# Even layer of a two-layer decoder: recurrent part first, value and gated outputs through DRAM, last head beside the output projection

## The chip, the cores and the metric

The kernel runs on one core of a Trainium2 chip. The metric is device time of one launch in microseconds (us), the median of several runs. Five engines work side by side, each through its own instruction stream in order: TensorE (PE, with its weight loads PEld), VectorE (DVE), ScalarE (ACT), GpSimd (POOL), and SyncE (SP), which here issues DMAs.

## The reference, cut to what matters

```python
# even layer, x: (1, 1024, 1024) f32
a_x, a_g, b_q, b_k, b_v, b_g = split(x @ w_in)           # 6 x 1024 columns
a_h = rg_lru(causal_dwconv(a_x, conv_w, conv_b), ...)    # gates: 8 blocks of 128x128, then a scan over the sequence
y_a = a_h * silu(a_g)
o_b = stick_breaking(b_q, b_k, b_v)                      # 8 heads of 128, strictly causal
y_b = o_b * silu(b_g)
x = layer_norm(alpha * x + concat([y_a, y_b]) @ w_out)
# odd layer: sliding-window attention, gated, output projection, layer norm (not touched by the change)
```

## The kernel before, in words

Every large product is made in three float32r passes (`mm3`, lines 109 to 112: high x high, high x low, low x high), so each operand exists as a high and a low tile. A "split" is an ACT copy that rounds to the high tile and a DVE subtraction that leaves the low one (`split_psum`, line 117). Weight pieces of 256 KB come by `load_piece` (line 91): one DMA on SP, then two POOL operations (lines 102 and 103) that split it. There are 3 raw and 5 split buffers for pieces.

The input x arrives transposed in 16 DMAs (`load_x`, line 124) and stays as 16 of the 24 `slots` of 4 KB per partition. The even layer has three stages:

1. **Attention**, heads n = 0 to 7 (`attn_all`, line 240). A head is 12 units (row tile i, key half g). `u_stage` makes the logits in a PSUM bank "z", ACT two sigmoids, DVE a reversed product scan and a product; `t_stage` transposes the weights on PE and splits them; `v_stage` multiplies them by the head's values. After each unit the loop pumps a *filler*: a generator of projection matmuls for the next head (`head_proj`, line 231: k, q, on even heads the values of two heads, then the gate), at a rate given by hand (line 325). `v_proj` (line 211) computes values 256 columns wide, for two heads at a time. Head 7's filler is `lru_proj(0)`.
2. **Recurrent part (LRU)**, blocks f = 0 to 7 (lines 468 to 473). `lru_main(f)` (line 402) makes two gates on PE, then Tanh, Exp, Sqrt on ACT, products on POOL and DVE, and a scan on DVE; `lru_proj(f+1)` (line 370: two projections, the depthwise convolution on DVE at line 381) is its filler.
3. **Output projection** (`out_proj`, line 483): for each half dm of the columns, 16 weight pieces e (8 of y_b, 8 of y_a), each against 8 row tiles s, accumulated in all 8 PSUM banks (3 "pj", 2 "z", 2 "tr", 1 "pv"). Ahead of it every y is split (lines 586 to 606; for y_b 1 to 7 the high part is made on POOL, line 590). The residual `xpre` (4 MB) is loaded at line 582.

The program text isn't the order on the engines: a planner of the framework takes every instruction with its dependences, buffers and a cost model, and writes each engine's order from a simulated run, first ready and earliest in the text first. Releases of buffers become semaphore waits. The profile's granted clock tells which of TensorE's two levels (1.2 and 2.4 GHz) holds.

Of the kernel before, what the change touches and what calls it, by code (L numbers as in the profile page):

```python
# [18 lines left out]
P = 128  # L19
# [33 lines left out]
def trunk(ctx, tc, x, xT_in, w_even, w_even_v, w_even_out, w_gate, lru_vec,  # L53
# [70 lines left out]
    def load_x(hf, dps):  # L124
        for dp in dps:
            raw = slot(f"xraw{hf}{dp}", F32)
            h = slot(f"xh{hf}{dp}", F32R)
            l = slot(f"xl{hf}{dp}", F32R)
            for c in range(2):
                x_dma.append(nc.sync.dma_start(raw[:, c, :], xT_in[hf, dp, :, c, :]))  # L130
                order(x_dma[-1], x_dma[-2] if len(x_dma) > 1 else None)
                nc.scalar.copy(h[:, c, :], raw[:, c, :])
                nc.vector.tensor_tensor(out=l[:, c, :], in0=raw[:, c, :], in1=h[:, c, :].bitcast(F32),  # L133
                                        op=ALU.subtract)
            xth[hf, dp], xtl[hf, dp] = h, l
# [45 lines left out]
    YB = {"vh": 3, "vl": 3, "wt": 2}  # L181
# [29 lines left out]
    def v_proj(pr, eng="pool", after=None):  # L211
        pieces = [load_piece(w_even_v[pr, g], f"v{pr}_{g}", eng=eng, after=after) for g in range(4)]
        for j in range(2):
            vt[2 * pr + j] = tuple(yt(f"v{c}", [P, NS, P], f"v{c}{2 * pr + j}") for c in "hl")
        for st in range(NS):
            ps = bank("pj", f"pjv_{pr}_{st}")[:, :256]
            for d in range(ND):
                wh, wl = pieces[d // 2]
                c = (d % 2) * 256
                xh, xl = xs(st // 4, d)  # L220
                c2 = (st % 4) * P
                mm3(ps, xh[:, c2:c2 + P], xl[:, c2:c2 + P], wh[:, c:c + 256], wl[:, c:c + 256],
                    d == 0, d == ND - 1)
                if d < ND - 1:
                    yield C_256
            for j in range(2):
                vh, vl = vt[2 * pr + j]
                split_psum(ps[:, j * P:(j + 1) * P], vh[:, st, :], vl[:, st, :])
            yield C_256

    def head_proj(n):
        yield from proj_ftile(w_even, 8 + n, f"k{n}", evac_qk("k", n), (1, 0))
        yield from proj_ftile(w_even, n, f"q{n}", evac_qk("q", n), (1, 0))
        if n % 2 == 0:
            yield from v_proj(n // 2)
        yield from proj_ftile(w_even, 16 + n, f"g{n}", evac_gate(("b", n)))

    rate = [0.0]

    def attn_all():  # L240
# [50 lines left out]
        def v_stage(n, j):  # L291
# [110 lines left out]
    def lru_main(f):  # L402
        st = lru_state[f]
        gh, gl = load_piece(w_gate[f], f"gate{f}", cols=256)
        if f < 6:
            ya = yt(YA[f], [P, 2, HALF], f"ya{f}", F32)
        else:
            if f == 6:
                ya67.append(yt("wt", [P, 2, 2, HALF], "ya67", F32))
            ya = ya67[0][:, f - 6]  # L410
        ytile["a", f] = ya
# [23 lines left out]
        for hf in range(2):  # L435
# [6 lines left out]
            nc.vector.tensor_tensor(out=ya[:, hf, :], in0=xc, in1=st["gg", hf], op=ALU.mult)  # L442
        yield

    getk = w_ftile(w_even, 8, "k0", "act", lazy=True)
    getq = w_ftile(w_even, 0, "q0", "act", lazy=True)
    load_x(0, [0])
    getk(0)
    load_x(0, [1])
    getk(4)  # L450
    load_x(0, [2, 3])
    getq(0)
    getq(4)
    load_x(1, range(4))
    for hf in range(2):
        for _ in proj_half(getk, hf, "k0", evac_qk("k", 0)):
            pass
        for _ in proj_half(getq, hf, "q0", evac_qk("q", 0)):
            pass
    for _ in v_proj(0, "act", x_dma[-1]):  # L460
# [6 lines left out]

    for f in range(8):
        if f + 1 < 8:
            fill.add(lru_proj(f + 1))  # L470
        for _ in lru_main(f):
            fill.pump(20.8 / 4)
        fill.drain()
# [5 lines left out]
    ACC = ["pv", "pj", "pj", "pj", "z", "z", "tr", "tr"]  # L479
# [3 lines left out]
    def out_proj(w_src, es, yh, n_tail, tail_piece, lnp, gb, after, name, final):  # L483
# [100 lines left out]
    yhl = {}

    def split_y(key, mk, pool_h=False):
        raw = ytile[key]
        h, l = mk(0, f"yh{key[0]}{key[1]}"), mk(1, f"yl{key[0]}{key[1]}")
        if pool_h:
            nc.gpsimd.tensor_scalar(out=fl(h), in0=fl(raw), scalar1=1.0, scalar2=0.0, op0=ALU.mult, op1=ALU.add)  # L590
        else:
            nc.scalar.copy(fl(h), fl(raw))
        nc.vector.tensor_tensor(out=fl(l), in0=fl(raw), in1=fl(h).bitcast(F32), op=ALU.subtract)
        yhl[key] = (h, l)
# [3 lines left out]
    for f in range(8):
        if f < 4:
            split_y(("a", f), lambda i, nm: slot(nm, F32R))  # L600
        else:
            if f == 4:
                ysp = yt("wt", [P, 2, 2, HALF], "yhla4")
                split_y(("a", f), lambda i, nm: ysp[:, i])
            else:
                split_y(("a", f), lambda i, nm, f=f: yt(YSPLIT[f][i], [P, 2, HALF], nm))

    def yh_even(e, s):
        h, l = yhl[("b", e - 8) if e >= 8 else ("a", e)]
        c = (s % 4) * P  # L610
        return h[:, s // 4, c:c + P], l[:, s // 4, c:c + P]
# [232 lines left out]
    for p in range(PAIRS):  # L844
        split_y(("o", p), lambda i, nm: slot(nm, F32R))
# [62 lines left out]
```

## Time and profile before

| | us |
|---|---|
| median of 3 runs | 1294.53 (1293.71 to 1295.31) |
| span of the profiled execution | 1294.7 |
| PE / PEld busy in it | 1259.2 / 1077.1 |
| DVE / POOL / ACT busy in it | 792.5 / 566.5 / 563.7 |

The page gives no other time of the profiled execution than its span. PE's matmuls overlap each other in the pipeline (one lasts 0.39 us while the next starts 0.23 us later), so a stretch in which PE is "busy" throughout can still run more or fewer matmuls; the number of matmuls in a stretch (x...) tells how fast it went.

### The profile page before, as it was taken

To read this page: it belongs to the slowest core of one execution; us is meant where nothing else is said; L and a number is where in the kernel's file an instruction comes from. 1 tells how busy PE (TensorE), PEld (TensorE's weight loads), DVE (VectorE), ACT (ScalarE), POOL (GpSimd) and SP (SyncE) were. 2 spreads that over 40 slices of the span, in tenths; PEclk is the share of its full clock that TensorE was granted. 3 is DMA by queue.
4 is the path that set the end of the run, shared out by engine and by line. 5 is a ranking of instruction groups with operands and counts; after the bars stand their busy time and mean duration, and the time that the engine had idled before them with its cause. 6 is when DMAs were issued, how large, how long until landed. Compare 5 with 4: busy or idle time off the path is not lost.

```text
span 1294.7 us, 18487 instructions
## 1 busy us (share of the span) xinstructions
PE 1259.2 (97%) x6656; PEld 1077.1 (83%) x6656; DVE 792.5 (61%) x1693; ACT 563.7 (44%) x1219; POOL 566.5 (44%) x695
## 2 busy tenths in 40 slices
PE   7999999999999999999998899999999999999997
PEld 6988988898889888888776688888788888887886
DVE  6266455645564559577777931126457877778467
ACT  4134333333333335565556700013357777778400
POOL 0332243314322422556657763536445555556440
PEclk9999999999999999999999899999899999999999
DMA  6211011101110110111111052210111111111122
GB/s 204 58 41 33 25 49 34 33 17 50 33 34 24 50 37 13 37 46 46 44 49 41 25 219 64 70 29 26 49 33 33 34 34 34 33 34 40 35 90 98
DMA packets 33643, 64.15 MB, mean 50 GB/s; under 512 B 3984, under 2 KB 5392, under 8 KB 33296
## 3 DMA queue, kind: packets, MB, share of 16 engines
q1 hardware_dynamic: 32976, 61.92, 15.8%
q8 instruction: 53, 0.87, 0.3%
q10 hardware_dynamic: 576, 1.05, 0.3%
q14 instruction: 38, 0.31, 0.1%
HBM read 58.76 MB, written 4.19 MB: 49 GB/s over the span
## 4 chain that ended last, share of the span: by engine, by line
PE 80%; DVE 11%; ACT 4%; issue 3%; POOL 1%; DMA 1%; POOLq 0%; ACTq 0%; DVEq 0%
PE ope L110 4%; PE ope L112 4%; PE ope L111 4%; PE tr L283 2%; PE pjv L112 2%; PE pjv L111 2%; PE pjv L110 2%; PE pj_g L112 2%; PE pj_g L110 2%; PE pj_g L111 2%; PE pj_q L110 2%; PE pj_q L111 2%; PE pj_q L112 2%; PE pj_k L111 2%; PE pj_k L112 2%
## 5 line engine op out<-in xcount | busy, mean ns | idle before, releaser
L264 ACT ACTIVATE C<-z 128x512 f32<-128x512 f32 (+3 forms) x96 | 47.4, 494 | 130.2 <-DVE z L261 77.0
L756 POOL TENSOR_SCALAR S<-S,sm 128x256 f32<-128x256 f32 (+1 forms) x128 | 59.9, 482 | 77.8 <-DVE sm L754 30.0
L751 ACT ACTIVATE S<-S,sm 128x256 f32<-128x256 f32 (+1 forms) x128 | 62.6, 490 | 57.1 <-DVE sm L747 55.3
L501 ACT ACTIVATE rs<-mv,eps_t 128x1 f32<-128x1 f32 x16 | 4.7, 295 | 183.4 <-DVE mv L500 183.4
L492 DVE SCALAR_TENSOR_TENSOR xpre<-xpre,ope 128x512 f32<-128x512 f32 x16 | 10.8, 681 | 107.0 <-PE ope L112 107.0
L110 PE MATMUL pjv<-wh_v,xh 128*128 128x256 f32 x256 | 73.3, 286 | 0.0
L112 PE MATMUL pjv<-wh_v,xl 128*128 128x256 f32 x256 | 72.4, 283 | 0.0
L111 PE MATMUL pjv<-wl_v,xh 128*128 128x256 f32 x256 | 72.4, 283 | 0.0
L312 POOL TENSOR_TENSOR yb<-pvt,yb 128x128 f32<-128x128 f32 x32 | 15.8, 492 | 126.2 <-DVE pvt L311 110.0
L273 DVE TENSOR_TENSOR_SCAN C<-C,C,one 128x512 f32<-128x512 f32 x32 | 41.7, 1302 | 41.7 <-ACT C L264 41.7
L273 DVE TENSOR_TENSOR_SCAN C<-C,one 128x512 f32<-128x512 f32 (+1 forms) x64 | 54.7, 854 | 16.4 <-ACT C L264 16.3
L118 ACT CAST wt<-tr 128x512 fp32r<-128x512 f32 (+3 forms) x96 | 46.6, 486 | 40.7 <-PE tr L283 38.9
L275 DVE TENSOR_TENSOR B<-B,C 128x512 f32<-128x512 f32 (+3 forms) x96 | 57.3, 597 | 10.2 <-ACT pvt L309 0.5
L261 DVE TENSOR_TENSOR z<-z,mask 128x128 f32<-128x128 f32 x64 | 18.8, 296 | 67.6 <-PE z L259 65.7
L102 POOL TENSOR_SCALAR wh_g<-wr_g 128x512 fp32r<-128x512 f32 x16 | 10.7, 668 | 111.3 <-PE pjv L112 42.6
L110 PE MATMUL pj_k<-xh,wh_k 128*128 128x512 f32 x128 | 52.7, 412 | 5.6 <-DVE wh_k L105 5.6
L119 DVE TENSOR_TENSOR wt<-tr,wt 128x512 fp32r<-128x512 f32 (+3 forms) x96 | 52.6, 549 | 7.9 <-ACT wt L118 7.6
L110 PE MATMUL pj_ag<-xh,wh_ag 128*128 128x512 f32 x128 | 51.8, 405 | 5.7 <-DVE xc L381 5.7
L110 PE MATMUL ope<-wh_e,yhb 128*128 128x512 f32 x128 | 51.2, 403 | 6.2 <-DVE gg L395 3.8
L110 PE MATMUL pj_oq<-x1h,wh_oq 128*128 128x512 f32 x128 | 52.8, 412 | 0.0
L111 PE MATMUL pj_k<-xl,wh_k 128*128 128x512 f32 x128 | 51.2, 400 | 1.3 <-DVE xl L133 1.3
L110 PE MATMUL pj_q<-xh,wh_q 128*128 128x512 f32 x128 | 52.0, 406 | 0.1
(300 smaller groups left out, 4541.0 us busy)
## 6 DMA issues: line engine op xcount, KB each, us to landing
wr_e<-in_w_even_out_dram SPq DMA_DIRECT2D x32, 256.0 KB, 2.6
xraw<-in_xT_dram SPq DMA_DIRECT2D x16, 256.0 KB, 5.0
wr_v<-in_w_even_v_dram SPq DMA_DIRECT2D x16, 256.0 KB, 2.6
wr_g<-in_w_even_dram SPq DMA_DIRECT2D x16, 256.0 KB, 2.6
wr_ax<-in_w_even_dram SPq DMA_DIRECT2D x16, 256.0 KB, 2.6
wr_ag<-in_w_even_dram SPq DMA_DIRECT2D x16, 256.0 KB, 2.6
xpre<-in_x_dram SPq DMA_DIRECT2D x8, 512.0 KB, 8.2
wr_oq<-in_w_odd_dram SPq DMA_DIRECT2D x16, 256.0 KB, 2.6
```

Of the source, the lines that this page charges most:

```text
L110: nc.tensor.matmul(ps, wh, xh, start=start, stop=False)
L111: nc.tensor.matmul(ps, wh, xl, start=False, stop=False)
L112: nc.tensor.matmul(ps, wl, xh, start=False, stop=stop)
L118: nc.scalar.copy(h, ps)
L119: nc.vector.tensor_tensor(out=l, in0=ps, in1=h.bitcast(F32), op=ALU.subtract)
L261: nc.vector.tensor_tensor(out=z[:, W - P:W], in0=z[:, W - P:W], in1=mask, op=ALU.add)
L264: nc.scalar.activation(C[:, :W], z[:, :W], AF.Sigmoid, scale=-SC)
L273: nc.vector.tensor_tensor_scan(cr, cr, one.broadcast_to([P, W]), init, ALU.mult, ALU.mult)
L275: nc.vector.tensor_tensor(out=B[:, :W], in0=B[:, :W], in1=C[:, 1:W + 1], op=ALU.mult)
L283: nc.tensor.transpose(tr[:, t * P:(t + 1) * P], B[:, t * P:(t + 1) * P], ident)
L751: nc.scalar.activation(Sb[:, j, lo:], Sb[:, j, lo:], AF.Exp, bias=nm[:, j:j + 1], accum_out=den[:, j:j + 1])
L756: nc.gpsimd.tensor_scalar(out=Sb[:, j, lo:], in0=Sb[:, j, lo:], scalar1=rec[:, j:j + 1], scalar2=0.0, op0=ALU.mult, op1=ALU.add)
```

## The change

The even layer is turned round. It starts with x and half of the value weights (now 512 columns wide, 8 loads of 256 KB, split on ACT and DVE in slots) and computes the values of heads 0 to 3 for row tiles 0 to 3 in four banks, as x arrives. Then come `lru_proj(0)` and the eight LRU blocks; their filler is `lru_proj(f+1)` and, 12 tiles in all, the other value tiles (`VT`), for block 7 the projections of head 0. Values go, split, to DRAM scratch (16 stores of 512 KB); y_a is split per half and stored (16 of 512 KB). Then the attention: every head's filler is k, q, gate of the next head; `load_v` fetches its values in 16 DMAs of 64 KB (rows of 512 bytes). y_b is split per half as it comes; heads 0 to 4 store it (10 of 512 KB), 5 to 7 keep it. In head 7 the 16 halves of y_a are loaded into the slots that x left, and the filler is `early_out`: 10 pieces against row tiles 0 to 2 of the first half of the output projection, in the three "pj" banks. The projection then loads those 10 pieces again for row tiles 3 to 7, and does the other 6 pieces for all; y_b 0 to 4 are loaded ahead of it.

```diff
-    def load_x(hf, dps):
...
+    def load_x(hf, d):
+        dp, c = d // 2, d % 2
...
+        raw = wt_(("kh", "kl")[c], f"xraw{hf}{d}", F32)
+        x_dma.append(nc.sync.dma_start(raw, xT_in[hf, dp, :, c, :]))
+        order(x_dma[-1], x_dma[-2] if len(x_dma) > 1 else None)
+        h, l = xs(hf, d)
+        nc.scalar.copy(h, raw)
+        nc.vector.tensor_tensor(out=l, in0=raw, in1=h.bitcast(F32), op=ALU.subtract)
-    YB = {"vh": 3, "vl": 3, "wt": 2}
+    YB = {"vh": 2, "vl": 2, "wt": 2}
-    def v_proj(pr, eng="pool", after=None):
...
+    vst = [[tc.dram_tile([P, 2, 4, P], F32, name=f"vst{q}{st}") for st in range(NS)] for q in range(2)]
+    def load_wv(q, d):
+        raw = wt_(("qh", "ql")[d % 2], f"wvraw{q}{d}", F32)
+        x_dma.append(nc.sync.dma_start(raw, w_even_v[q, d]))
...
+        hl = wv[q, d] = slot(f"wv{q}{d}", F32R)
+        nc.scalar.copy(hl[:, 0, :], raw)
+        nc.vector.tensor_tensor(out=hl[:, 1, :], in0=raw, in1=hl[:, 0, :].bitcast(F32), op=ALU.subtract)
+    def v_evac(ps, q, st):
+        hl = yt(("vh", "vl")[st % 2], [P, 2, HALF], f"vhl{q}{st}")
+        split_psum(ps, hl[:, 0, :], hl[:, 1, :])
+        nc.sync.dma_start(vst[q][st].rearrange("p a h f -> p a (h f)"), hl.bitcast(F32))
+    def v_tiles(q, sts):
+        for st in sts:
+            ps = bank("pv", f"pjv{q}_{st}")
+            for d in range(ND):
+                v_mm(ps, q, st, d)
+                yield C_512
+            v_evac(ps, q, st)
+    def load_v(n):
+        vt[n] = tuple(yt(f"v{c}", [P, NS, P], f"v{c}{n}") for c in "hl")
         for st in range(NS):
+            for i in range(2):
+                nc.sync.dma_start(vt[n][i][:, st, :].bitcast(F32), vst[n // 4][st][:, i, n % 4, :])
     def head_proj(n):
...
-        if n % 2 == 0:
-            yield from v_proj(n // 2)
+    def split_y_half(key, hf, raw, keep):
+        hl = slot(f"yhl{key[0]}{key[1]}{hf}", F32R) if key[0] == "b" else \
+            yt(("vh", "vl")[hf], [P, 2, HALF], f"yhla{key[1]}{hf}")
+        nc.scalar.copy(hl[:, 0, :], raw)
+        nc.vector.tensor_tensor(out=hl[:, 1, :], in0=raw, in1=hl[:, 0, :].bitcast(F32), op=ALU.subtract)
+        if keep:
+            yhl[key + (hf,)] = hl
+        else:
+            yst[key + (hf,)] = tc.dram_tile([P, 2, HALF], F32, name=f"yst{key[0]}{key[1]}{hf}")
+            nc.sync.dma_start(yst[key + (hf,)], hl.bitcast(F32))
@@ attn_all
                     if n + 1 < SB_HEADS:
+                        load_v(n + 1)
                         fill.add(head_proj(n + 1))
-                        rate[0] = (31.2 if (n + 1) % 2 else 52.0) / 12
+                        rate[0] = 31.2 / 12
                     else:
-                        decay()
-                        fill.add(lru_proj(0))
-                        rate[0] = 20.8 / 12
+                        for hf in range(2):
+                            for f in range(8):
+                                load_y(("a", f), hf, slot(f"yla{f}{hf}", F32R))
+                        fill.add(early_out())
+                        rate[0] = 20.4 / 12
@@ lru_main
-            nc.vector.tensor_tensor(out=ya[:, hf, :], in0=xc, in1=st["gg", hf], op=ALU.mult)
+            nc.vector.tensor_tensor(out=gg, in0=xc, in1=gg, op=ALU.mult)
+            split_y_half(("a", f), hf, gg, False)
+    EARLY = [13, 0, 1, 2, 3, 4, 5, 6, 7, 14]
+    LATE = [8, 9, 10, 11, 12, 15]
+    for d in range(ND):
+        load_x(0, d)
+        load_wv(0, d)
+    ps = [bank(VB[st], f"pjv0_{st}") for st in range(4)]
+    for d in range(ND):
+        for st in range(4):
+            v_mm(ps[st], 0, st, d)
...
+    VT = [(0, (4, 5)), (0, (6, 7)), (1, (0,)), (1, (1, 2)), (1, (3,)), (1, (4,)), (1, (5, 6)), (1, (7,))]
+    for f in range(8):
+        q, sts = VT[f]
+        if f == 2:
+            for d in range(ND):
+                load_wv(1, d)
+        fill.add(v_tiles(q, sts))
+        if f + 1 < 8:
+            fill.add(lru_proj(f + 1))
+        else:
+            load_v(0)
+            fill.add(head_proj(0))
...
-    ACC = ["pv", "pj", "pj", "pj", "z", "z", "tr", "tr"]
+    ACC = ["pj", "pj", "pj", "z", "z", "tr", "tr", "pv"]
@@ out_proj: dm == 0 goes on from the three early banks
+                for ei, group in enumerate(early[1:]):
+                    for idx, e in enumerate(group):
+                        wh, wl = load_piece(w_src[dm, e], f"{name}{dm}_{e}")
+                        for s in range(NS):
+                            if ei == 0 and s in early[0]:
+                                continue
...
-    for n in range(8):
-        split_y(("b", n), lambda i, nm: slot(nm, F32R), n > 0)
...
```

## Rows read from the trace of the kernel before

**Rows 1.** The page: busy time per engine, and the span in 40 slices.
```profile
PE 1259.2 (97%) x6656; PEld 1077.1 (83%) x6656; DVE 792.5 (61%) x1693; ACT 563.7 (44%) x1219; POOL 566.5 (44%) x695
...
PE   7999999999999999999998899999999999999997
...
PEclk9999999999999999999999899999899999999999
```

**Rows 2.** PE in order of time: last half projections, then values of head 0.
```profile
26.21 0.39 PE L110 MATMUL pj_k<-xh,wh_k 128*128 128x512 f32 x1
...
31.66 0.28 PE L110 MATMUL pjv<-wh_v,xh 128*128 128x256 f32 x1
...
34.53 0.63 PE L257 MATMUL z<-kh,qh 128*128 128x512 f32 x2
```

**Rows 3.** Busy time (instructions), granted clock, DMA share and GB/s of stretches, us.
```profile
175.00:225.00 50.00, 50.00 (x270) 42.78 (x269) 27.33 (x56) 17.26 (x41) 18.01 (x26) 1.00 0.17 48
...
550.00:625.00 75.00, 75.00 (x333) 62.12 (x332) 56.28 (x68) 43.36 (x57) 44.65 (x38) 1.00 0.17 48
625.00:750.00 125.00, 109.85 (x446) 86.98 (x445) 101.36 (x99) 79.81 (x96) 88.93 (x65) 0.95 0.13 38
750.00:850.00 100.00, 100.00 (x442) 82.82 (x442) 16.28 (x21) 1.06 (x1) 47.94 (x49) 1.00 0.35 116
...
760.00:765.00 5.00, 5.00 (x23) 4.13 (x22) 0.00 (x0) 0.00 (x0) 0.84 (x1) 1.00 1.02 415
```

**Rows 4.** The chain of waits through the LRU stage, in order of time.
```profile
614.42 0.67 DVE xc L381
...
642.14 0.67 DVE xc L381
...
669.78 0.67 DVE xc L381
...
697.46 0.67 DVE xc L381
```

**Rows 5.** PE in order of time at the end of the LRU stage, with its waits.
```profile
711.71 0.50 PE L111 MATMUL g<-xcl,wh_gate 128*128 128x512 f32 x1 [3.09 <-DVE xcl L389]
...
722.48 0.50 PE L110 MATMUL ope<-wh_e,yhb 128*128 128x512 f32 x1 [3.81 <-DVE gg L395]
...
733.83 0.80 PE L110 MATMUL ope<-wh_e,yhb 128*128 128x512 f32 x1 [2.00 <-ACT ri L420]
734.42 0.63 PE L111 MATMUL ope<-wl_e,yhb 128*128 128x512 f32 x1
734.85 0.63 PE L112 MATMUL ope<-wh_e,ylb 128*128 128x512 f32 x1
```

**Rows 6.** Groups of instructions by line, DVE and ACT, shapes apart.
```profile
L389 DVE TENSOR_TENSOR xcl<-xc,xch 128x512 fp32r<-128x512 f32 x16 | 19.5, 1219 | 8.9 <-ACT xch L388 8.9
L119 DVE TENSOR_TENSOR kl<-pj_k,kh 128x512 fp32r<-128x512 f32 x16 | 10.9, 682 | 0.1
L133 DVE TENSOR_TENSOR xl<-xraw,xh 128x512 fp32r<-128x512 f32 x16 | 10.8, 683 | 0.5 <-ACT xh L132 0.5
...
L132 ACT CAST xh<-xraw 128x512 fp32r<-128x512 f32 x16 | 9.8, 622 | 9.9 <-DMA xraw<-in_xT_dram 9.5
```

**Rows 7.** PE in order of time at the start, with its waits.
```profile
5.64 0.77 PE L110 MATMUL pj_k<-xh,wh_k 128*128 128x512 f32 x1 [5.64 <-DVE wh_k L105]
6.88 0.80 PE L111 MATMUL pj_k<-xl,wh_k 128*128 128x512 f32 x1 [0.47 <-DVE xl L133]
...
13.82 0.50 PE L111 MATMUL pj_k<-xl,wh_k 128*128 128x512 f32 x1 [0.80 <-DVE xl L133]
```

**Rows 8.** SP in order of time: DMA issues of the first 24 us.
```profile
0.74 0.86 SPq L130 DMA_DIRECT2D xraw<-in_xT_dram  x2
1.65 0.42 SPq L344 DMA_DIRECT2D vec<-in_lru_vec_dram  x1
2.12 12.22 SPq L130 DMA_DIRECT2D xraw<-in_xT_dram  x12
22.54 0.33 SPq L654 DMA_DIRECT2D sp<-in_sinks_dram  x1
22.91 0.91 SPq L130 DMA_DIRECT2D xraw<-in_xT_dram  x2
```

**Rows 9.** DVE and ACT in order of time at the end of head 7.
```profile
520.97 0.49 DVE L261 TENSOR_TENSOR z<-z,mask 128x128 f32<-128x128 f32 x2
...
524.25 0.29 DVE L275 TENSOR_TENSOR B<-B,C 128x128 f32<-128x128 f32 x1
...
522.47 0.31 ACT L265 ACTIVATE B<-z 128x128 f32<-128x128 f32 x1
```

**Rows 10.** Groups by line, POOL: the split of an output-projection piece.
```profile
L103 POOL TENSOR_TENSOR wl_e<-wr_e,wh_e 128x512 fp32r<-128x512 f32 x29 | 43.1, 1488 | 1.9
...
L102 POOL TENSOR_SCALAR wh_e<-wr_e 128x512 fp32r<-128x512 f32 x29 | 22.6, 781 | 52.8 <-PE ope L112 41.6 <-DMA wr_e<-in_w_even_out_dram 11.1
```

**Rows 11.** DMA issues: KB each, median us from issue to landing.
```profile
xpre<-in_x_dram SPq DMA_DIRECT2D x8, 512.0 KB, 8.2
...
wr_gate<-in_w_gate_dram SPq DMA_DIRECT2D x8, 128.0 KB, 2.0
```

More of the change, by code (lines that the diff above doesn't have):

```diff
@@ L122, in trunk @@
     x_dma = []
-    def load_x(hf, dps):
[L125 to L135, printed above, removed]
+    def load_x(hf, d):
+        dp, c = d // 2, d % 2
+        if c == 0:
+            xth[hf, dp], xtl[hf, dp] = slot(f"xh{hf}{dp}", F32R), slot(f"xl{hf}{dp}", F32R)
+        raw = wt_(("kh", "kl")[c], f"xraw{hf}{d}", F32)
[4 more added lines that the diff above has]
+        nc.vector.tensor_tensor(out=l, in0=raw, in1=h.bitcast(F32), op=ALU.subtract)
     def xs(hf, d):
@@ L312, in v_stage @@
             nc.gpsimd.tensor_tensor(out=y[:, P:], in0=tmp, in1=y[:, P:], op=ALU.mult)
+            if j % 2 == 0:
+                split_y_half(("b", n), j // 2, ytile["b", n][:, j // 2, :], n >= KEPT)
         LAG = 2
@@ L452, in trunk, with yh_even @@
[L452 to L460, printed above, removed]
-        pass
-    for _ in proj_ftile(w_even, 16, "g0", evac_gate(("b", 0))):
-        pass
+    def yh_even(e, s):
+        hl = yhl[("b", e - 8, s // 4) if e >= 8 else ("a", e, s // 4)]
+        c = (s % 4) * P
+        return hl[:, 0, c:c + P], hl[:, 1, c:c + P]
@@ new lines, in trunk, with early_out @@
+    EARLY = [13, 0, 1, 2, 3, 4, 5, 6, 7, 14]
+    LATE = [8, 9, 10, 11, 12, 15]
+    op0 = {}
+    def early_out():
+        for s in range(3):
+            op0[s] = bank("pj", f"ope0_{s}")
+        for idx, e in enumerate(EARLY):
+            wh, wl = load_piece(w_even_out[0, e], f"f0_{e}")
+            for s in range(3):
+                yh_, yl_ = yh_even(e, s)
+                mm3(op0[s], yh_, yl_, wh, wl, idx == 0, False)
+                yield C_512
+    VB = ["z", "z", "tr", "tr"]
+    for d in range(ND):
+        load_x(0, d)
+        load_wv(0, d)
@@ L466, in trunk @@
     fill.drain()
[L468 to L473, printed above, removed]
     wk_ctx.close()
@@ L477, in trunk, with out_proj @@
     xpre = xp.tile([P, NS, D], F32, name="xpre")
-    ACC = ["pv", "pj", "pj", "pj", "z", "z", "tr", "tr"]
+    ACC = ["pj", "pj", "pj", "z", "z", "tr", "tr", "pv"]
     LNC = 768
-    def out_proj(w_src, es, yh, n_tail, tail_piece, lnp, gb, after, name, final):
+    def out_proj(w_src, es, yh, n_tail, tail_piece, lnp, gb, after, name, final, early=None):
         def parts(s):
@@ L543, in out_proj @@
             body = es[:len(es) - nt]
+            if dm == 0 and early:
+                ps = dict(early[0])
+                for ei, group in enumerate(early[1:]):
[4 more added lines that the diff above has]
+                                continue
+                            if s not in ps:
+                                ps[s] = bank(ACC[s], f"op{name}{dm}_{s}")
+                            yh_, yl_ = yh(e, s)
+                            mm3(ps[s], yh_, yl_, wh, wl, ei == 0 and idx == 0, e == early[-1][-1])
+                body = []
             for idx, e in enumerate(body):
@@ L580, in trunk @@
     nc.sync.dma_start(gb, e_ln.rearrange("(o a) d -> o a d", o=1).broadcast_to([P, 2, D]))
+    for n in range(4):
+        if n < 2:
+            ysp = yt("wt", [P, 2, 2, HALF], f"ylb{n}")
+            yb_ = [ysp[:, 0], ysp[:, 1]]
+        else:
+            yb_ = [yt("vh" if n == 2 else "vl", [P, 2, HALF], f"ylb{n}{hf}") for hf in range(2)]
+        for hf in range(2):
+            load_y(("b", n), hf, yb_[hf])
+    for hf in range(2):
+        load_y(("b", 4), hf, slot(f"ylb4{hf}", F32R))
     for s in range(NS):
         nc.sync.dma_start(xpre[:, s, :], x[s * P:(s + 1) * P, :])
[L584 to L594, printed above, removed]
-    for n in range(8):
-        split_y(("b", n), lambda i, nm: slot(nm, F32R), n > 0)
[L598 to L611, printed above, removed]
     x1h, x1l = {}, {}
@@ L844, in trunk @@
     for p in range(PAIRS):
-        split_y(("o", p), lambda i, nm: slot(nm, F32R))
+        raw = ytile["o", p]
+        h, l = slot(f"yho{p}", F32R), slot(f"ylo{p}", F32R)
+        nc.scalar.copy(fl(h), fl(raw))
+        nc.vector.tensor_tensor(out=fl(l), in0=fl(raw), in1=fl(h).bitcast(F32), op=ALU.subtract)
+        yhl["o", p] = (h, l)
     def yh_odd(e, s):
```

65 lines of the change are left out of this document (28 added, 37 removed).

## The prediction, made before the changed kernel was run

> **What bounds the kernel now.** I read the page first: PE is busy 97% of the span, DVE 61% [rows 1], so only PE's own work and PE's gaps can be worth anything. Because a busy PE may be a slow one, I then counted matmuls per stretch. In steady state 24 matmuls of 512 columns take 31.66 - 26.21 = 5.45 us, 0.2272 us each; 24 of 256 columns take 34.53 - 31.66 = 2.87 us, 0.1196 us each [rows 2]. In the attention (175 to 225 us) PE is full while DVE works 27 us of 50; from 550 to 625 us and from 750 to 850 us PE runs at pitch (333 x 0.2272 = 75.7 us of 75; 442 x 0.2272 = 100.4 us of 100). Between, from 625 to 750 us, it ran 446 matmuls, 101.3 us of work in 125: 23.7 us lost, at a granted clock of 0.95 [rows 3].
>
> Why there: a block of the LRU stage has 96 + 12 matmuls, 24.5 us, but the chain of waits through DVE, ACT and POOL comes round every 27.7 us (614.42, 642.14, 669.78, 697.46) [rows 4]. PE first lives on its lead, then waits. At the end of the stage no projection is left to run, and the output projection cannot start for want of banks and split y: waits of 3.09, 3.81 and 2.00 us, and after the last PE runs at 0.43 us a matmul, the lower of its two clock levels [rows 5].
>
> **The change, part by part.** All sums start from the profiled span, 1294.7 us, 0.2 us above the median of the runs.
>
> *LRU stage.* The 12 value tiles of 24 matmuls and head 0's 144 matmuls become its filler. PE's work: 7 blocks x 24.5 + block 7's 12 + 144 matmuls (35.4) + 12 x 5.45 (65.4) = 272.6 us. The chain: 8 x 27.7 = 222 us, plus two y_a splits a block and 1.5 value splits on average. A subtraction with an operand in PSUM costs 0.68 us; the y_a one reads two SBUF tiles, and the nearest row, the one of this stage (xcl), took 1.22 us on average against 0.68 for xl at the start, when POOL was idle [rows 6]. I take 1.22: a block's chain becomes 27.7 + 2.4 + 1.0 = 31.1 us, in all 249 us; by 0.68 it would be 30.1. Both are under PE's 272.6, so PE becomes the bound. The Trainium skill (SBUF — State Buffer, Who interferes with whom) says the same of that row: a DVE instruction with two SBUF inputs contends with a GpSimd one that reads SBUF. Block by block it is closer: blocks with one tile hold PE 30.0 us, and block 2 adds 8 weight splits (8 x 0.68 = 5.5 us of DVE) to the chain, 36 us against 30, which block 3 with 35.4 us makes good only in part. So of the 23.7 us I give back 3 here (bounds 0 and 12: 8 x 1.5) and 1 at the handover to head 0, where the 27.7 us chain of block 7 has 35.4 us of PE beside it. The POOL and DVE splits of y_b that crowded the old handover are spread over the heads. Net -19.7.
>
> *Value width.* 768 matmuls of 256 columns become 384 of 512: 384 x (2 x 0.1196 - 0.2272) = 4.6 us less PE work [rows 2]. Net -4.6. The attention's PE work is otherwise moved, not changed.
>
> *Start.* Before, the first matmul began at 5.64 us and PE waited 0.47 and 0.80 us more for x [rows 7]. Now both operands of the first matmul come from ACT, one copy (0.62) later; then each of 8 steps brings 512 KB for 12 matmuls, 2.73 us, against 2 issues, 1.24 us on ACT and 1.37 us on DVE. SP sends vec and sinks, which stand hundreds of lines later, ahead of the last x loads [rows 8]: ready DMAs pass waiting ones in the planner's order, so I expect the second half of x ahead of the value stores. -1 (bounds -2 and +3).
>
> *Attention.* Heads 0 to 6 have the filler that odd ones had (their stretch in rows 3 is PE-full). Added per head: two halves split (2 x 0.62 ACT, 2 x 0.68 to 1.22 DVE), on engines half idle: 0. `load_v`: 16 issues at about 0.45 us (two took 0.91 [rows 8]) = 7 us of SP and 1 MB. It lands while the head before runs: 0, if SP isn't held; if it is, see the third rival.
>
> *Last head and tail.* After head 7's last logits (mask at 520.97) DVE finished its weights at 524.5 [rows 9]; transposes, a split and two value products follow, so "tr" and "pv" come free some 8 us after the last logits. "z" is free after the sigmoids (522.8), about 2 us in; 5 pieces x 2 row tiles x 3 matmuls = 6.8 us of output projection can fill the rest. I take 3 lost (0 to 8, the larger if the clock drops as in rows 5).
>
> *Transfers.* From head 7's start to the end of the 10 repeated pieces SP brings 8.4 MB of y_a, 20 pieces (5.2), 5.2 MB of y_b, xpre and gb (5.2) and first late pieces (1.6): 25.6 MB. PE has 20.4 + about 15 (the head's own matmuls, from columns at the pitches of rows 2) + 150 x 0.2272 = 69.5 us for it. At the 415 GB/s of the xpre burst [rows 3] it needs 62 us. It fits, but pieces queue behind bursts: y_b, xpre and gb together hold the DMA engines 25 us, and 5 buffered pieces cover 5 x 15 x 0.2272 = 17. I take 3 (0 to 29: both bursts uncovered, 20.5 + 8.5). The Trainium skill (DMA: Bandwidth & Descriptors, Where 436 GB/s comes from) puts HBM to SBUF at about 358 GB/s a core; the row exceeds it, and the measurement decides. By the page the same bytes would take an estimated 71.5 us, 2 us more than PE has. POOL's split of a piece, 0.78 + 1.49 = 2.27 us [rows 10], fits into the 3.4 us that five row tiles hold PE.
>
> Sum: 1294.7 - 19.7 - 4.6 - 1 + 3 + 3 = 1275.4; forecast **1275**.
>
> **The rivals.** *The chain still binds:* PE's order is fixed by the planner's costs; if its waits fall within the blocks, the stage gives back 12 us rather than 4, and the tail 8 rather than 3: 1288. For it: block 2, and single-tile blocks, whose chain with splits at 1.22 us (27.7 + 2.4 + 0.7 = 30.8) is longer than PE's 30.0. Against: 24 us of slack in the sum. 0.18.
>
> *The bursts:* weight pieces wait behind y_a at head 7's start (8.4 MB, 20.5 us) and behind y_b, xpre and gb (8.5 us uncovered); 29 rather than 3: 1301 at worst, 1288 with half of it. For it: one FIFO on SP, and PE's order is fixed before the run. Against: the old xpre burst at 760 us cost PE nothing [rows 3]. 0.12.
>
> *SP held, slower than before:* `load_v(n+1)` stands ahead of head n+1's weight pieces, and its buffers (two each of "vh" and "vl") come free only after head n-1's last `v_stage`, two or three units, some 10 us, into head n. If SP takes it in that order, k and q weights come up to 10 + 7 us late in each of seven heads, and units without filler leave PE empty. At 5 us a head it is 35: 1310. It decides from about 3 us a head, where the gain of 19 is eaten. A 64 KB load is no obstacle itself: 128 KB landed in 2.0 us [rows 11]. Against it, the order in rows 8. 0.12. If instead the early output projection found no place beside head 7, 20 us of PE work would only move behind it: inside the first rival's price.
>
> **How the numbers follow.** The forecast has 0.58, with a range of its own of 1263 (nothing given back: 1294.7 - 23.7 - 4.6 - 2 = 1264) to 1284. The range 1262 to 1297 takes in the chain and the bursts up to their worst, and leaves out the held SP and the far end of the bursts, about 0.16. About 0.2%, 2.6 us, is what a measurement of this kernel can tell from no change. Faster: the forecast, 0.16 of the chain, 0.04 of the bursts, 0.78. Same: 0.02 and 0.06, 0.08. Slower: 0.02 of the bursts and the held SP, 0.14.
>
> **What would show it.** In the changed profile: PE at pitch (about 110 matmuls per 25 us) through the LRU stage; 384 value matmuls of 512 columns; no PE wait of over 2 us between the stages but one of a few us at head 7's end; 25 to 30 us with the DMA share near 1 around it. Wrong would be: PE waiting for POOL's weight splits at the start of each head (SP held), for DVE's xc or xcl in the LRU stage (chain), or for y_a, y_b or pieces in head 7 and after it (bursts).

## The result, and the profile after

The changed kernel takes 1277.19 us (median of four, 1275.71 to 1278.42) against 1294.33 (1293.71 to 1295.31) in the same comparison: a ratio of 0.9867, 95% interval 0.9853 to 0.9881, so 1.3% faster. The profiled execution took 1275.71 us at a span of 1273.7, so about 2.0 us lie around a span. The span fell by 21.0 us and the median by 17.1: the profiled execution of before was a long one of its kernel, by 2.4 us if the same 2.0 lie around its span, and that of after a short one, by 1.5. Of what follows, sums in spans stand against 21.0; the time itself fell by 17.1.

The page of the changed kernel, the rows that answer to [rows 1]:

```profile
PE 1246.3 (98%) x6272; PEld 1052.6 (83%) x6272; DVE 770.1 (60%) x1661; ACT 577.9 (45%) x1212; POOL 542.4 (43%) x692
...
PE   8999999999999999999999979999999999999997
...
PEclk9999999999999999999999989999999999999999
DMA  7322332234212222123128571201111111111022
```

The dent of [rows 1] at the slices of the LRU stage, with the clock down beside it, is gone. One new slice stands out, the 24th (732 to 764 us), at the end of three slices of heavier DMA. Stretches of the changed kernel, with the columns of [rows 3]: the LRU stage with its filler, heads 0 to 7, head 7's end, the gap, and the output projection.

```profile
20.00:300.00 280.00, 278.01 (x1223) 229.05 (x1222) 162.24 (x248) 148.47 (x201) 122.66 (x121) 1.00 0.32 106
330.00:700.00 370.00, 369.85 (x2009) 317.36 (x2008) 247.58 (x473) 152.89 (x354) 117.84 (x176) 1.00 0.28 90
700.00:740.00 40.00, 39.93 (x203) 33.12 (x202) 17.31 (x31) 10.19 (x24) 23.68 (x28) 1.00 0.63 222
740.00:755.00 15.00, 8.40 (x27) 6.45 (x26) 0.00 (x0) 0.00 (x0) 5.77 (x7) 0.78 0.69 256
755.00:850.00 95.00, 95.00 (x420) 78.58 (x420) 14.69 (x27) 2.94 (x4) 42.09 (x43) 1.00 0.23 63
```

From 20 to 300 us, 1223 matmuls at the 0.2272 us of [rows 2] are 277.9 us of work in 280: about 2 lost where [rows 3] lost 23.7. Heads and head 7's end are full. From 740 to 755 us, 27 matmuls are 6.1 us of work in 15: about 9 lost. PE's waits of the whole run (line, waited for: us in total, times, longest):

```profile
PE ope L110 <- POOL wh_e L102: 6.6, 1, 6.6
PE pjv L110 <- ACT wv L219: 6.2, 2, 4.7
```

The second is the start (4.7) and 1.5 us in block 2 of the LRU stage. The first is the gap. PE in order of time around it:

```profile
742.82 0.39 PE L112 MATMUL ope<-wh_e,yla 128*128 128x512 f32 x1
749.82 2.50 PE L110 MATMUL ope<-wh_e,yla 128*128 128x512 f32 x5 [6.60 <-POOL wh_e L102]
752.12 0.63 PE L111 MATMUL ope<-wl_e,yla 128*128 128x512 f32 x1
752.54 0.63 PE L112 MATMUL ope<-wh_e,yla 128*128 128x512 f32 x1
```

SP, which issues the loads:

```profile
724.26 1.75 SPq L267 DMA_DIRECT2D ylb<-ystb  x4
726.05 0.53 SPq L645 DMA_DIRECT2D gb<-in_e_ln_dram  x1
...
728.15 9.86 SPq L658 DMA_DIRECT2D xpre<-in_x_dram  x7
739.00 20.66 SPq L93 DMA_DIRECT2D wr_e<-in_w_even_out_dram  x8
```

POOL, which splits the pieces:

```profile
749.14 0.62 POOL L102 TENSOR_SCALAR wh_e<-wr_e 128x512 fp32r<-128x512 f32 x1 [13.12 <-DMA wr_e<-in_w_even_out_dram]
```

The DMA engines from 720 to 755 us in 40 slices of 0.875 us, busy tenths and GB/s:

```profile
DMA  8999818998999999999999999999999951003606
GB/s 243 393 386 342 330 33 300 328 375 281 337 398 454 393 440 407 389 435 398 431 426 407 403 403 417 407 412 403 412 405 386 386 218 47 0 0 80 211 9 124
```

SP sent six y_b halves, gb and the residual x (xpre) ahead of the next weight piece of the output projection. Those are 15 loads, 8.4 MB; the DMA engines are full from 727 to 748 us, and the piece, issued at 739.00, is there for POOL at 749.14. In the chain of waits that ended last, its flight is one line:

```profile
739.00 9.99 DMA wr_e<-in_w_even_out_dram
```

PE had used up its buffered pieces at 743. After its 6.60 us of idleness it first ran at 0.42 us a matmul (752.12 to 752.54), the lower of its two clock levels; the stretch's granted clock is 0.78. Of the 9 us 6.6 are the idle time; most of the rest is that lower clock.

The other terms. At the start the first matmul now begins at 4.69 us (5.64 in [rows 7]), ACT and PE in order of time:

```profile
3.37 0.62 ACT L132 CAST xh<-xraw 128x512 fp32r<-128x512 f32 x1 [1.35 <-DMA xraw<-in_xT_dram]
...
4.69 2.07 PE L110 MATMUL pjv<-wv,xh 128*128 128x512 f32 x4 [4.69 <-ACT wv L219]
```

And the handover to the odd layer, where the x1 transposes wait for the layer norm, ran at a fuller clock than before. Stretches, before first, after second:

```profile
910.00:915.00 5.00, 3.13 (x8) 2.45 (x8) 3.75 (x5) 1.47 (x3) 5.00 (x6) 0.63 0.06 12
915.00:920.00 5.00, 5.00 (x19) 3.94 (x19) 0.97 (x2) 0.00 (x0) 4.52 (x7) 0.69 0.47 145
```

```profile
890.00:895.00 5.00, 2.50 (x10) 1.67 (x11) 4.74 (x7) 1.93 (x5) 5.00 (x5) 1.00 0.00 0
895.00:900.00 5.00, 5.00 (x30) 4.30 (x29) 2.07 (x4) 2.35 (x5) 4.60 (x8) 1.00 0.51 147
```

From the last output-projection matmul to the last x1 transpose it is 25.2 us before and 22.3 after.

Where the 21.0 us came from, each worked out as the time of a stretch less its matmuls at the pitches of [rows 2]: start -3.7, LRU stage about -21 (23.7 lost before, 2 to 3 after), value width -4.6, gap about +9, handover -2.9. That is -23.2; a loss of about 2 lies elsewhere and isn't placed.

### The profile page after: what moved, and what is told of

Same layout as the page of the kernel before. It is cut to its first block, busy times and chain, and to the rows that moved or that the text cites. A ratio compares the mean times of both kernels' runs of the same rounds, so it can differ in the third digit from the quotient of the medians.

```text
span 1273.7 us, 18009 instructions
## 1 busy us (share of the span) xinstructions
PE 1246.3 (98%) x6272; PEld 1052.6 (83%) x6272; DVE 770.1 (60%) x1661; ACT 577.9 (45%) x1212; POOL 542.4 (43%) x692
## 4 chain that ended last, share of the span: by engine, by line
PE 83%; DVE 6%; ACT 5%; DMA 2%; issue 2%; POOL 1%; SPq 0%; POOLq 0%; ACTq 0%; DVEq 0%
PE ope L110 4%; PE ope L112 4%; PE ope L111 4%; PE tr L315 2%; PE pj_g L110 2%; PE pj_g L111 2%; PE pj_g L112 2%; PE pjv L110 2%; PE pjv L111 2%; PE pjv L112 2%; PE opo L111 2%; PE opo L110 2%; PE opo L112 2%; PE pj_k L112 2%; PE pj_k L111 2%; PE pj_q L110 2%
## 5 line engine op out<-in xcount | busy, mean ns | idle before, releaser
L110 PE MATMUL pjv<-wv,xh 128*128 128x512 f32 x128 | 49.6, 399 | 6.2 <-ACT wv L219 6.2
L110 PE MATMUL pj_g<-xh,wh_g 128*128 128x512 f32 x128 | 51.9, 406 | 0.4 <-DVE kl L119 0.4
L791 DVE CUSTOM_DVE_ANT_0 S<-s,bias 128x256 f32<-128x256 f32 (+1 forms) x128 | 47.4, 403 | 7.7 <-PE s L786 6.9
L110 PE MATMUL pj_og<-x1h,wh_og 128*128 128x512 f32 x128 | 51.9, 406 | 0.0
L112 PE MATMUL pj_k<-xh,wl_k 128*128 128x512 f32 x128 | 51.6, 403 | 0.0
L111 PE MATMUL pj_og<-x1l,wh_og 128*128 128x512 f32 x128 | 51.0, 398 | 0.0
L111 PE MATMUL pjv<-wv,xh 128*128 128x512 f32 x128 | 50.5, 394 | 0.5 <-DVE wv L220 0.5
L112 PE MATMUL pj_og<-x1h,wl_og 128*128 128x512 f32 x128 | 50.8, 397 | 0.0
```

The lines of the kernel that those rows point to most:

```text
L110: nc.tensor.matmul(ps, wh, xh, start=start, stop=False)
L111: nc.tensor.matmul(ps, wh, xl, start=False, stop=False)
L112: nc.tensor.matmul(ps, wl, xh, start=False, stop=stop)
L791: nc.vector.tensor_tensor_reduce(out=Sb[:, j, lo:], in0=ps[:, j, lo:], in1=bias[:, j, lo:], scale=1.0, scalar=-BIG, op0=ALU.add, op1=ALU.m ...
```

## The experiments

Two theories of the gap stood against each other: the order in which SP issues (the residual burst ahead of the piece), and the amount of data. Three more questions were what the filler and the wide value matmuls are worth, and whether the output projection beside head 7 matters.

**Residual loaded behind the third late piece.**

```diff
+                        if (ei, idx) == (1, 2):
+                            load_xpre(pdma[-1])
...
-    for s in range(NS):
-        nc.sync.dma_start(xpre[:, s, :], x[s * P:(s + 1) * P, :])
+    def load_xpre(last):
+        for s in range(NS):
+            order(nc.sync.dma_start(xpre[:, s, :], x[s * P:(s + 1) * P, :]), last)
+        order(nc.sync.dma_start(gb, ...), last)
```

> The residual loads (xpre, 4 MB) and gb (1 MB) are issued behind the third of the six late weight pieces, not ahead of the repeated early ones; nothing else changes. Theory (bursts): in the changed kernel PE stood 6.6 us for a weight piece that lay behind y_b, gb and xpre in SP's queue and in the DMA engines, and then ran about 11 matmuls at 0.43 us; both go, 9.3 us less in the span, 1273.7 to about 1264.5, and no PE wait over 2 us at the end of head 7. Rival (the tail itself): the wait comes from head 7's end or from POOL's splitting, so it stays whatever is loaded; 1273.7 within 2.5. Second rival (bytes): the 5.2 MB only move the wait behind them; PE stands as long some 20 us later, 1273 to 1277.

Measured: 1268.89 us, ratio 0.9799 (0.9785 to 0.9814), span 1267.2. The gap's stretch:

```profile
740.00:755.00 15.00, 15.00 (x68) 12.41 (x67) 0.00 (x0) 0.00 (x0) 6.88 (x7) 1.00 0.77 282
```

68 matmuls in place of 27, 41 x 0.2272 = 9.3 us more work, with the wait gone and the clock at 1.00; the DMA engines carry as much. So the whole gap was the piece standing behind the residual and gb. The same piece is now issued at 734.23 and lands 2.60 us later, in place of 739.00 and 9.99 us: some 6 us of its delay were the order of issue (this run is 1.3 us late there), some 7 the full DMA engines. The span fell by 6.5 only: the first logits came 1.3 us later and the handover to the odd layer took 24.0 us, 1.7 more than in the changed kernel.

**Residual on ACT's queue.**

```diff
-        nc.sync.dma_start(xpre[:, s, :], x[s * P:(s + 1) * P, :])
+        nc.scalar.dma_start(xpre[:, s, :], x[s * P:(s + 1) * P, :])
```

(gb likewise.)

> The same loads stay where they are in the text but are issued by ACT instead of SP. If the order of issue on SP holds the weight pieces (one queue, SP waiting between the residual issues), the pieces pass and most of the 9.3 us go: span about 1265 to 1267. If it is the DMA engines' backlog alone, 10 MB at 415 GB/s ahead of the piece, the piece lands as late as before: 1273.7 within 2.5.

Measured: 1276.43 us, ratio 0.9858 (0.9841 to 0.9874), span 1273.6: no gain. PE's wait in the gap, and SP's longest between 720 and 752 us:

```profile
PE ope L110 <- POOL wh_e L102: 5.6, 1, 5.6
...
SPq L93 <- DMA ylb<-ystb: 14.4, 1, 14.4
```

SP's queue and ACT's in order of time:

```profile
724.91 3.12 SPq L267 DMA_DIRECT2D ylb<-ystb  x6
742.52 17.06 SPq L93 DMA_DIRECT2D wr_e<-in_w_even_out_dram  x8
...
726.84 13.93 ACTq L658 DMA_DIRECT2D xpre<-in_x_dram  x8
```

SP had nothing left ahead of the piece and still waited 14.4 us for a y_b half to land; that half, issued at 727.71, was there at 742.45, while the DMA engines were full. Why SP waits for that half stands in the trace's records: each DMA names one of eight semaphores (counters that tell when it has landed), which SP's and ACT's DMAs take in turn together, and the program issues none before the DMA that had its semaphore last has landed. The piece got the semaphore of that y_b half, with seven residual loads between them in the turn. So on ACT's queue the residual still stood ahead of the piece, and the run can't tell whether a piece that is issued at once would pass the burst. It shows that moving the burst to the other queue gains nothing here; issuing it later does. The y_b loads stayed on SP, so their share of the wait isn't told apart from the residual's.

**All value tiles before the LRU stage** (the LRU stage without filler).

```diff
-            ps = bank("pv", f"pjv{q}_{st}")
+            ps = bank(("z", "z", "tr", "tr")[st % 4], f"pjv{q}_{st}")
...
+    for _ in v_tiles(0, (4, 5, 6, 7)):
+        pass
+    for d in range(ND):
+        load_wv(1, d)
+    for _ in v_tiles(1, range(NS)):
+        pass
     decay()
...
-        fill.add(v_tiles(q, sts))
-        r = (5.2 * len(sts) + (20.8 if f < 7 else 31.2)) / 4
+        r = (20.8 if f < 7 else 31.2) / 4
```

> The 12 value tiles that fill the LRU blocks are computed ahead of the LRU stage instead, over four banks; blocks 0 to 6 keep only the next block's projections as filler, block 7 those of head 0. Same PE work. Theory (the chain was the bound, the value tiles fill it): each block falls back to its chain, 27.7 us plus two y_a splits at 0.75 to 1.2 us, 29 to 30 us, against 24.5 of PE: seven blocks lose 4.7 to 5.5 us, 33 to 39 us; with 3 us for the second half of the value weights and less some lead of PE, the span rises to 1297 to 1312. Rival (the gain of the change comes from the handover to the output projection, which no longer lies behind the LRU stage, not from the filler): within 5 of 1273.7.

Measured: 1296.72 us, ratio 1.0014 (1.0004 to 1.0023), span 1292.9: 19.2 more than the changed kernel, all of its gain, though less than the 1297 to 1312 expected. The first logits come 16.6 us later (342.0 in place of 325.4). A stretch of the stage:

```profile
175.00:325.00 150.00, 136.98 (x577) 110.87 (x576) 109.13 (x132) 91.70 (x120) 91.25 (x76) 0.97 0.25 80
```

PE's largest wait:

```profile
PE pj_ag L110 <- DVE xc L414: 12.2, 5, 3.6
```

The chain of waits in order of time:

```profile
181.88 0.67 DVE xc L414
...
210.29 0.67 DVE xc L414
...
238.67 0.67 DVE xc L414
```

The chain's period is 28.4 us (210.29 - 181.88, 238.67 - 210.29), with the 24.5 us of PE work that the prediction counts beside it, and PE waits for it again. So the filler is what the LRU term is worth. The chain is 0.7 us a block longer than in [rows 4], not the 2.4 that the prediction adds for y_a; that is net of two changes, since the two y_a splits come in at 0.711 us each on average and the two of xcl fall from 1.219 to 0.710.

**Value matmuls of 256 columns again.**

```diff
-            for d in range(ND):
-                v_mm(ps, q, st, d)
-                yield C_512
+            for c0 in (0, 256):
+                for d in range(ND):
+                    v_mm(ps, q, st, d, slice(c0, c0 + 256))
+                    yield C_512 / 2
```

> The 12 value tiles of the LRU stage are made in two halves of 256 columns: 288 matmuls of 512 become 576 of 256. Theory (PE is the bound in that stage): 288 x (2 x 0.1196 - 0.2272) = 3.5 us longer, span about 1277, and the stage from 20 to 300 us 3.5 us longer. Rival (the stage is still held by the DVE chain, the width is hidden): within 1 of 1273.7.

Measured: 1282.4 us, ratio 0.9901 (0.9887 to 0.9916), span 1280.8, 7.1 more. The stretch with all 12 tiles of the filler:

```profile
20.00:305.00 285.00, 282.36 (x1511) 244.17 (x1510) 161.81 (x245) 148.77 (x201) 121.62 (x120) 1.00 0.30 102
```

12 tiles of 24 matmuls become 576 narrow ones in place of 288: 288 x (2 x 0.1196 - 0.2272) = 3.5 us, as reckoned. The first logits came 5.5 us later (3.5 of work by that sum; of the rest 0.7 is the start, 58 matmuls begun by 20 us in place of 61), and the handover to the odd layer took 24.0 us in place of 22.3. The narrow matmuls cost time, so PE is the bound there; the whole difference is twice the work term, and the handover's part has nothing to do with the width.

**No output projection beside head 7** (on the kernel with the late residual).

```diff
-                        fill.add(early_out())
-                        rate[0] = 20.4 / 12
...
-                ps = dict(early[0])
+                ps = {}
```

> On the kernel with the late residual (span 1267.2): head 7 gets no filler, the three early banks and their 30 piece-by-row-tile products are gone, and the first half of the output projection does all 16 pieces for all 8 row tiles after the attention. Same PE work, ten weight pieces less to load. Theory (the early output projection fills a head whose own PE work is about 15 us): head 7 runs at its DVE and ACT chain, 26 to 32 us in place of the 37 us it takes with its filler, and 20.4 us of PE work follow it: 10 to 16 us longer, span 1277 to 1283. Rival (head 7's chain takes 36 us anyway): 20 us longer, 1287. Second rival (the planner finds other work, the projection's own pieces, for the gaps of head 7): within 3 of 1267.2.

Measured: 1269.49 us, ratio 0.9802 (0.9788 to 0.9817), span 1266.3: the same as with it. PE's matmuls of the output projection (tile ope: PE, PEld, DVE, clock, DMA share, GB/s) within head 7, without the early part:

```profile
674.00:702.00 28.00, 11.89 (x45) 8.00 (x45) 0.00 (x0) 1.00 0.90 346
```

With it (the kernel with the late residual):

```profile
673.00:710.00 37.00, 21.54 (x81) 14.33 (x81) 0.00 (x0) 1.00 0.77 291
```

The logits of all heads (line L292: first and last start), without, then with:

```profile
L292 PE MATMUL z<-kh,qh x96: 222/389/419, 327.2 to 701.7; 128*128 128x512 f32 x48, 128*128 128x384 f32 x16, 128*128 128x256 f32 x16, 128*128 128x128 f32 x16
```

```profile
L292 PE MATMUL z<-kh,qh x96: 221/389/423, 326.7 to 709.5; 128*128 128x512 f32 x48, 128*128 128x384 f32 x16, 128*128 128x256 f32 x16, 128*128 128x128 f32 x16
```

The output projection comes into head 7 either way, 45 matmuls in place of 81, as the second rival had it: the planner moves ready work up by itself. The logits take 374.5 us in place of 382.8, 8.3 us less, for 36 x 0.2272 = 8.2 us of output projection that run behind them. That the early part gains nothing in the changed kernel either is shown by the next run but one.

**In block 2, the value tile behind the next projection** (on the kernel with the late residual), to close the gap of 1.5 us.

```diff
-        fill.add(v_tiles(q, sts))
+        if f != 2:
+            fill.add(v_tiles(q, sts))
         if f + 1 < 8:
             fill.add(lru_proj(f + 1))
+            if f == 2:
+                fill.add(v_tiles(q, sts))
```

> On the kernel with the late residual (span 1267.2): in LRU block 2 alone the projection of block 3 stands ahead of the value tile in the filler. Theory: the one PE gap of the LRU stage, about 3 us near 129 us, is that tile waiting for the ACT and DVE splits of the second half of the value weights, which are loaded in that block; later in the filler it finds them split: 2 to 3 us less, span about 1264.5. Rival (that block's DVE chain, with 8 more splits, is the bound): the gap moves into the block's projections, 1267.2 within 1.

Measured: 1276.09 us, ratio 0.9856 (0.984 to 0.9873), span 1273.8, 6.6 more. PE's largest wait:

```profile
PE pjv L113 <- DVE vhl L122: 8.5, 1, 8.5
```

The theory fell. All filler tiles share the one bank "pv"; now three stood in a row, and one had to wait until the tile before it was split off the bank, in DVE's queue behind the LRU chain. PE stood from 157 to 165 us and ran on at 0.43 us a matmul.

**No early output projection, on the changed kernel itself** (the edit of two runs back).

> The changed kernel with the residual loads where the change has them, and without the early output projection alone: no filler in head 7, no repeated pieces, all 16 pieces against 8 row tiles. Theory (cover): a piece now holds PE 24 matmuls, 5.45 us, so five buffered ones cover 27 us of the 25 us burst of y_b, gb and xpre; the 6.6 us wait and its slow matmuls go by that alone, and the planner brings output projection into head 7 by itself as in the run before: span 1266 to 1269. Rival (the burst must be moved, or it stalls PE whatever a piece holds): the wait stays, 1273 to 1276.

Measured: 1271.2 us, ratio 0.9828 (0.9813 to 0.9842), span 1271.3. PE's wait in the gap:

```profile
PE ope L110 <- POOL wh_e L102: 2.2, 1, 2.2
```

The gap's stretch:

```profile
735.00:750.00 15.00, 12.84 (x57) 10.32 (x56) 0.00 (x0) 0.00 (x0) 6.02 (x7) 1.00 0.68 251
```

With less of the projection done beside head 7, more is left to run while the burst passes: the wait shrinks from 6.6 to 2.2 us, but the burst still reaches past the buffered pieces. The profiled execution is the longest of its four: its span is only 2.4 us below the changed kernel's, since the first logits came 2.8 us later and the handover took 1.6 more, but the median is 6.0 us lower. So on the changed kernel the early part is no gain but a loss. That it draws down the pieces ahead of the burst fits both runs, and isn't shown further: with the residual moved away, leaving it out changed nothing.

**Three buffers of split weights instead of five** (on the run before), to see what SP's holding costs with less cover.

```diff
-    def load_piece(src, name, pool=None, hb=5, eng="pool", cols=HALF, q=None, after=None):
+    def load_piece(src, name, pool=None, hb=3, eng="pool", cols=HALF, q=None, after=None):
```

> The kernel of the run before with 3 split buffers for weight pieces in place of 5, everywhere. It asks why SP, held some 10 us by the value loads in each head, cost nothing. Theory (cover): with 3, pieces cover 16 us of pure projection and about 24 us beside a head's own matmuls, against a hold of up to 15 us and 7 us of 16 issues: the heads lose 0 to 3 us each, and the burst after head 7, 25 us against 16, about 9 us with its slow matmuls; span 1276 to 1295, with PE waiting for POOL's split of k or q pieces in the heads. Rival (the planner puts the value loads where they don't matter, buffers or not): PE waits in no head, and only the burst adds its 9 us: 1275 to 1278.

Measured: 1314.97 us, ratio 1.0165 (1.0148 to 1.0182), span 1313.4, 42.1 more than the run before. The stretch of the heads:

```profile
330.00:700.00 370.00, 368.38 (x1987) 315.75 (x1987) 247.92 (x477) 155.24 (x357) 112.41 (x174) 1.00 0.26 85
```

PE's largest wait, and SP's for the buffers of load_v (L245):

```profile
PE x1tr L670 <- DVE xpre L585: 21.8, 6, 13.8
...
SPq L245 <- PE pv L338: 60.0, 6, 14.8
```

SP is held for 60.0 us in six waits, as in the changed kernel (below), and PE is empty for 1.6 us of the heads' 370. So SP's holding costs next to nothing even with three buffers; one q piece was waited for, 2.6 us, ahead of head 0. The loss is elsewhere: the last logits come only 1.8 us later than in the run before, the last matmul of the output projection 7.5 (PE's wait in the gap is 5.1 us), the last x1 transpose 27.5, the first logits of the odd layer 38.9. The x1 transposes, which began at 858.9 us with the output projection going on to 878.6, now begin at 900.4, behind its end at 886.1. How the buffers bring that about was not followed further.

**Weight splits of block 2 on POOL** (on the kernel with both edits above, late residual and no early projection).

```diff
+        if q == 1:
+            nc.gpsimd.tensor_scalar(out=hl[:, 0, :], in0=raw, scalar1=1.0, scalar2=0.0, op0=ALU.mult, op1=ALU.add)
+            nc.gpsimd.tensor_tensor(out=hl[:, 1, :], in0=raw, in1=hl[:, 0, :].bitcast(F32), op=ALU.subtract)
+            return
```

> On the kernel with the late residual and without the early output projection (span 1266.3): the 8 splits of the second half of the value weights, in LRU block 2, go from ACT and DVE to POOL (one tensor_scalar and one tensor_tensor each, about 2 us). Theory (those splits stand in ACT's and DVE's queues behind the block's own chain, and the block's value tile waits for them): the gap of about 3 us near 130 us goes, POOL being idle half of the time there; span 1263 to 1264. Rival (POOL takes 16 us for them and holds the block's products and weight pieces): the gap stays or grows, 1266 to 1272.

Measured: 1276.94 us, ratio 0.9875 (0.9858 to 0.9891), span 1275.2, 8.9 more. PE's largest waits in the LRU stage:

```profile
PE g L113 <- ACT xch L426: 3.3, 1, 3.3
...
PE pjv L113 <- POOL wv L223: 1.7, 1, 1.7
PE pjv L113 <- DVE vhl L122: 1.7, 1, 1.7
```

This theory fell too, and the loss is beyond the rival's 1272: one wait of 1.5 us became three, of which only one is for POOL's splits. The other two are on ACT and DVE; that the planner's order for them changed is likely, but was not followed.

## Why the prediction was right, point by point

The forecast was 1275 with 1262 to 1297, and the kernel took 1277.19. The sum was made in spans (1275.4 against 1273.7 to 1276.3 measured); the 2.0 us around a span were not in it, and count for nearly all of the difference to the median. The total is right partly by luck, because errors cancel: against the sum, the LRU stage came out 1.3 us better, the start 2.7, the tail 3 and the handover 2.9, the transfers 6 worse, with about 2 not placed. The base of the sum was a long execution: by medians the gain was 17.1 us, and the sum has 19.3.

- *LRU stage*, -19.7: right in mechanism and size (about -21). PE is at 112 matmuls per 25 us from 25 to 125 us. That the filler does it is shown by the run without it, 19.2 us slower. Inside the term two sizes were off the safe way. The y_a split was taken at 1.22 us, the price of xcl before; it took 0.75, and xcl itself fell to 0.89:

```profile
L422 DVE TENSOR_TENSOR xcl<-xc,xch 128x512 fp32r<-128x512 f32 x16 | 14.2, 885 | 6.7 <-ACT xch L421 6.7
...
L259 DVE TENSOR_TENSOR yhla<-gg,yhla 128x512 fp32r<-128x512 f32 x16 | 12.0, 749 | 1.5 <-ACT yhla L258 1.4
```

  Both means mix two prices. Of the 16 y_a splits 15 took 0.68 to 0.69 us, with no POOL instruction beside them, and one that began under a POOL split took 1.72. What decides is which of the two is running when the other begins. In the kernel before, 9 of the 16 xcl rows began while a POOL instruction ran and took 1.04 to 1.80 us; the other 7 took 0.68 to 0.69. In the run with the values first, the same subtraction mostly began a little ahead of POOL's split and took 0.69, and in the pair below POOL paid (1.82 us for 1.29):

```profile
589.64 1.29 POOL L103 TENSOR_TENSOR wl_ax<-wr_ax,wh_ax 128x512 fp32r<-128x512 f32 x1
589.69 1.79 DVE L389 TENSOR_TENSOR xcl<-xc,xch 128x512 fp32r<-128x512 f32 x1 [0.74 <-ACT xch L388]
```

```profile
213.26 0.69 DVE L422 TENSOR_TENSOR xcl<-xc,xch 128x512 fp32r<-128x512 f32 x1 [0.74 <-ACT xch L421]
213.27 1.82 POOL L103 TENSOR_TENSOR wl_ax<-wr_ax,wh_ax 128x512 fp32r<-128x512 f32 x1
```

  The Trainium skill (SBUF — State Buffer, Who interferes with whom) says that a DVE instruction with two SBUF inputs contends with a GpSimd one that reads SBUF. The trace agrees: both rows are of that kind, and the one that began second was the longer. Block 2 was rightly named as the tight one: its weight splits are the stage's one wait, 1.5 us.
- *Value width*, -4.6: right in sign; the narrow run's first logits come 5.5 us later where the same working gives 3.5 for the 12 tiles of the filler.
- *Start*, -1: the step that the first matmul comes one ACT copy later was wrong. It came 0.95 us earlier, since ACT now does the first x copy at 3.37 and PE no longer waits for DVE's cast of a weight [rows 7]; after that the waits were 0.5 us. -3.7, beyond the bound of -2.
- *Attention*, 0: right, PE 369.85 of 370.
- *Last head and tail*, +3: 0. PE is full from 700 to 740 us. But not by the merit of the early output projection, which two runs show to be worth nothing or less: the order on the engines is the planner's, and it fills head 7's end with whatever is ready.
- *Transfers*, +3 with 8.5 for y_b, xpre and gb: this term was mis-sized. The burst and its place were right, and 8.5 was near the uncovered part (about 9 lost, 9.3 won back when the residual is moved), but partly by luck: its own 25 less 17 is 8, and of the 9 only 6.6 are idle time, the rest mostly the lower clock, which it didn't hold. I weighed it down to 3 because the bursts fit on the whole; it is the place that counts. The argument against it, that the old xpre burst cost nothing at 760 us, did not carry over to a burst with y_b ahead of it.
- *Handover to the odd layer*: not in the sum, -2.9. It took 25.2 us before, 22.3 after and in two of the experiments, 23.7 to 24.0 in six others with the same instructions. The granted clock goes with it: of its rows of 5 us two are low before (0.63 and 0.69), one with the late residual (0.68) and one in the narrow run (0.66), none in the changed kernel. Why the clock falls in one and not in the other is open.

The rivals: *the chain still binds* fell in the LRU stage. *The bursts* came true for one of its two, y_b with xpre and gb, with the sign that the prediction named, PE waiting for a piece behind head 7; y_a's 20 us at head 7's start were covered. *SP held* is half right: the mechanism is there (in the changed kernel, too, SP's queue stands at L245 for 60.0 us in six waits, the longest 14.8), and its price at PE is 0, since no k or q piece is waited for in the heads. The point from which I let it decide, 3 us a head, was never reached, not with three buffers either.

The best kernel of the study is the changed one with the residual loaded behind the third late piece: 1268.89 us, 0.9799 of before. Leaving the early output projection out of it as well changes nothing (1269.49).

## What to carry to other kernels

Before sending a burst of loads, ask which piece is next in line on the same DMA engines and how many microseconds of work are buffered ahead of it: a total that fits is no answer, and another issuing queue is no remedy where the program's DMAs take turns for the same semaphores. Give an engine-bound stage independent matmuls as filler and check the sum of the chain against the sum of the work; it was worth 19 us here. And don't take a contended instruction's price from a mean: look at single rows and at what was running when each began.

## What was not expected of the hardware

- At most eight transfers are out at a time, counted across queues. With the residual on ACT's queue, ACT's issues followed landings one by one (issued at 734.06 and 737.38, 0.02 us behind the landings, at 734.04 and 737.36, of y_b halves that SP had issued), and SP stood for 14.4 us with nothing ahead of its piece. In the changed kernel, SP alone issued the same way, 728.15 to 738.01 for seven loads. The program sets this: in the records of both traces DMAs take eight semaphores in turn (those of the y_b half that landed at 734.04 and of the load issued at 734.06 are the same), and none is issued before the last one with its semaphore has landed. Whether the chip has a limit of its own isn't shown.
- From 730 to 748 us, while the burst ran, the slices of 0.875 us moved 386 to 454 GB/s. The Trainium skill (DMA: Bandwidth & Descriptors, Where 436 GB/s comes from) puts HBM to SBUF at about 358 GB/s a core; that figure halves what two cores share, and only one ran here. The trace is above it, and the measurement decides.
- Behind the idle time of 6.60 us the matmuls ran at 0.42 us (752.12 to 752.54), in a stretch of granted clock 0.78. In the run with POOL's wait of 2.2 us the clock stayed at 1.00, but behind a wait of 2.00 us in the kernel before they ran at 0.43 [rows 5]: the length of one wait doesn't tell which level follows.
